# The last product of a hybrid decoder block: one more buffer at each step of its weight supply

## The chip, the cores and the metric

The kernel runs on one core of one Trainium2 chip. The metric is the device time of one execution in microseconds, and the time given is the median of several runs. Engines are named as the profile names them: PE (TensorE), DVE (VectorE), ACT (ScalarE), POOL (GpSimd) and SP (SyncE, which here only issues DMAs).

## What is computed

One decoder layer over 256 tokens and 2048 features in float32: three token mixers with gates, an output product `w_o`, and a feed-forward part. The stage that matters here is the last one of the reference:

```python
h = rms_norm(x, norm_ffn_pre[l])
u = causal_depthwise_conv(h @ w_up[l], ffn_conv_w[l], ffn_conv_b[l])
u_g, u_v = jnp.split(u, 2, axis=-1)
x = x + rms_norm((jax.nn.silu(u_g) * u_v) @ w_down[l], norm_ffn_post[l])
```

`w_up` is 2048 x 11264 and `w_down` is 5632 x 2048. "The up projection" is the product with `w_up`, "the last product" the one with `w_down`.

## The kernel before

**Numbers as pairs.** Each float32 weight is split into a rounded value and a rest: ACT writes the rounded one (`whi`, a copy to type fp32r), DVE subtracts it from the raw weight and writes the rest (`wlo`). A product of such pairs takes three matmuls: rounded by rounded, rest by rounded, rounded by rest. So every raw piece of 128 x 1024 weights goes by DMA into a raw buffer `wraw`, then through one ACT and one DVE instruction, and then feeds PE.

**The last product.** The 5632 rows of `w_down` are 44 tiles of 128. 24 of them (`PLAIN`) are multiplied as they are: a "plain" step loads one piece (1024 of the 2048 output columns), splits it, and issues 12 matmuls of 128x512. The other 20 form ten pairs (`EARLY`) that are multiplied with Strassen's scheme: a "quad" step loads two pieces `b` and `a`, forms a difference piece `t` and a half piece of further differences with DVE, splits all of these (three and a half pieces), and issues 7 x 3 = 21 matmuls. It does everything twice, once for each half of the output columns (`Pair(0)`, `Pair(1)`): 2 x (24 x 12 + 10 x 21) = 996 matmuls. A quad is 8 DVE instructions, 4 ACT instructions and 2 DMAs; a plain step is one of each.

**Order.** In the last product ACT and DVE run in the order in which the code issues their instructions (`fixed` chains each to the one before on its engine), and PE too (`in_line`). `high` is the ACT rounding, `rest` the DVE subtraction (both show as line L980, that of `fixed`; the matmuls are L1264). The surrounding tile framework orders the tail of the up projection against this chain. DMAs of weights are issued by SP in one queue, in order; an issue waits until the buffer that it fills has been read for the last time.

**Buffers.** The pool `P0` holds 5 raw buffers (`wraw`), 4 rounded ones (`whi`) and 4 rests (`wlo`), used in turn; the half piece of a quad has its own two tiles (`h4`, `l4`). A big tile with tag `hT` in `P0` holds first `hT`, then pieces of `w_o`, then `h2T` (the activations of the up projection, 16 x 2 x 256 numbers in each partition), and in the last product `fin`: the result rows, a row of gains, and two scratch pieces for `t`. The small tiles of the up projection's activation (`t`, `fs`, `fa`) lie in a pool `P2b`, which is closed at the end of the up projection; the pool `P2c` is opened in its place.

**Steps of the two halves.** With P a plain step and Q a quad, the loops before give for the first half PPPQ, nine times PPQ, and PPP. In the second half the last six plain pieces are kept: they are loaded and split early, but multiplied at the very end (K). Its order is PPP, the results of the first half, Q PQ PPQ PPQ PQ PPQK PPQK PQK PPQK PPQ KK, with weighing steps and a gain load between. The kept pieces of the quads go to tiles of the activations that are no longer read.

After the last product follow the row norm, the residual and the output DMAs.

Of the kernel before, what the change touches and what calls it, by code (L numbers as in the profile page):

```python
# [23 lines left out]
F32 = mybir.dt.float32  # L24
# [6 lines left out]
D = 2048  # L31
T = 256
# [3 lines left out]
EPS = 1e-6  # L36

EARLY = [(0, 1), (2, 3), (4, 5), (6, 7), (8, 9), (11, 12), (13, 14), (15, 16), (17, 18), (19, 20)]
PLAIN = [*range(22, 33), 10, 21, *range(33, NFT)]
BA, BB, BC, BG = 2100, 2200, 2200, 2500  # L40
PR = 1000
NW0, _ = 9, 6
# [12 lines left out]
def block(ctx: ExitStack, tc: tile.TileContext, x, xf, fp, cst, rows, sgw, w1, w2, wf_a, wt_bv, wf_bu, wf_c,  # L55
# [3 lines left out]

    PZ = ctx.enter_context(tc.tile_pool(name="pz", bufs=1))  # L60
    P0 = ctx.enter_context(tc.tile_pool(name="p0", bufs=1))
    PS = ctx.enter_context(tc.tile_pool(name="ps", bufs=4, space=PSUM))
    marks = set()

# [687 lines left out]
    class Unit:  # L752
# [251 lines left out]
    for cb in range(3):  # L1004
# [7 lines left out]
        if cb < 2:  # L1012
            for t in range(2):
                done_o(cb, t)
    h2k = P0.tile([128, 4, 2, 1024], R, tag="hT", name="h2k")
# [10 lines left out]
    for n, (cb, p) in enumerate(HELD):  # L1026
        for i in range(2):
            if n == 0 and i == 0:
                pe_last[0] = mm_o(cb, 1, p, held[n], (i,))
            else:  # L1030
                in_line(mm_o, cb, 1, p, held[n], (i,))
            if (n, i) == (3, 1):
                h2 = P0.tile([128, KT, 2, T], R, tag="hT", name="h2T")
            k = 2 * n + i - 7
            if k == 14:
                order_of(order2)
                fixed(S, S.activation, junk, po[3, 1], AF.Square, accum_out=ss1[1][:, 3:4])
            for k in ([k] if 0 <= k < 14 else [14, 15] if k == 14 else []):
                in_line(enter2, 0, k)
                if k % 4 == 3:  # L1040
                    up = wf_up[k // 8][:, k // 4 % 2 * 1024:k // 4 % 2 * 1024 + 1024]
                    if k < 15:
                        behind.append(tuple(order2))
                        ws2[k // 8].append(piece(up, 1024))
                    else:
                        raw = fetch(up, 1024)
        if p == 7 and cb == 2:
            done_o(cb, 1)
# [170 lines left out]
    turn = [0]  # L1219

    def scratch():
        turn[0] ^= 1
# [9 lines left out]
    def high(hi, x):  # L1232
        fixed(S, S.activation, hi, x, AF.Copy)

    def rest(lo, x, hi):
        fixed(V, V.tensor_sub, lo, x, hi.bitcast(F32))

    def weights(src, into=None):
        raw = fetch(src, 1024)
        hi, lo = (into[:, 0], into[:, 1]) if into is not None else ring(raw.name)  # L1240
        high(hi, raw)
        rest(lo, raw, hi)
        return hi, lo

    def ring(name):
        return [P0.tile([128, 1024], R, tag=tag, bufs=4, name=f"{tag}{name}") for tag in ("whi", "wlo")]

    class Pair:
        def __init__(self, p):
# [25 lines left out]

        def quad(self, j):

            k0, k1 = EARLY[j]
            last = j == len(EARLY) - 1
            b, a = (fetch(wt_dq[self.p, j][:, x:x + 1024], 1024) for x in (0, 1024))  # L1280
            L, U = slice(0, 512), slice(512, 1024)
            nm = f"q{self.p}_{j}"
            tt = scratch()
            (hb, lb), (ha, la), (ht, lt) = (ring(nm + x) for x in "bat")
            h4, l4 = (P2c.tile([128, 512], R, tag=tag, name=f"{tag}{nm}") for tag in ("h4", "l4"))
            high(hb, b)
            fixed(V, V.tensor_sub, tt[:, L], b[:, L], a[:, U])
# [3 lines left out]
            fixed(V, V.tensor_sub, tt[:, U], b[:, L], a[:, U])  # L1291
            high(ht, tt)
            rest(la, a, ha)
            fixed(V, V.tensor_sub, b[:, U], b[:, U], tt[:, U])
            high(h4[:, L], b[:, U])
            rest(lt, tt, ht)
            rest(l4[:, L], b[:, U], h4[:, L])
            sh, sl = sums_at(j)
            s1, s2, s4 = ((sh[:, i], sl[:, i]) for i in range(3))
            for bank_, act, (h, l), c in (  # L1300
                    (self.c[0][1], s4, (hb, lb), L), (self.c[0][0], g2(k1, H1), (hb, lb), U),
                    (self.p1, g2(k0, H1), (ha, la), L), (self.p5, s1, (ha, la), U),
                    (self.p7, g2(k0, H2), (ht, lt), L), (self.p6, s2, (ht, lt), U),
                    (self.c[1][0], g2(k1, H2), (h4, l4), L)):
# [34 lines left out]
    NP, NQ, KEEP = len(PLAIN), len(EARLY), 6  # L1339


    first, second = Pair(0), None
    i = 0
    for j in range(NQ):
        while i < 3 + (NP - 6) * j // (NQ - 1):
            first.plain(i)
            i += 1
        first.quad(j)
    for i in range(i, NP):
        first.plain(i)  # L1350
    first.combine()
    second = Pair(1)
    kept = []
    i = 0
    for j in range(NQ):
        while i < 3 + (NP - KEEP - 3) * j // (NQ - 1):
            second.plain(i)
            if i == 2:
                for t in range(2):
                    for n in range(2):  # L1360
                        first.result(t, n, fixed)
            elif 3 <= i < 7:
                first.weigh((i - 3) // 2, (i - 3) % 2, fixed)
            elif i == 9:
                nc.sync.dma_start(gain, row(3072, 1024))
            i += 1
        second.quad(j)
        if j == len(EARLY) - 1:
# [3 lines left out]
        for x in range(0 if j < NQ - 5 else 1 if j < NQ - 1 else KEEP - 4):  # L1372
            k = NP - KEEP + len(kept)
            into = None
            if j < NQ - 1:
                kt = P2.tile([128, 11, T], R, tag=("gh", "gl")[j % 2], bufs=4, name=f"kept{k}")
                into = kt[:, 0:8].rearrange("p (a b) c -> p a (b c)", a=2)
            kept.append((PLAIN[k], weights(wt_dn[1, k], into)))
    assert i == NP - KEEP and len(kept) == KEEP
    second.combine()  # L1380
    for t in range(2):
        for n in range(2):
# [21 lines left out]
def _layout(inp):  # L1404
# [66 lines left out]
    k0, k1 = [k for k, _ in EARLY], [k for _, k in EARLY]  # L1471
    quads = np.concatenate([dn[:, k1, 1], dn[:, k1, 0], dn[:, k0, 0], dn[:, k0, 1]], axis=3)


# [40 lines left out]
```

## Time and profile before

| | |
|---|---|
| median of 3 runs | 1578.02 us (1577.71 to 1579.3) |
| the profiled execution, its time | 1579.86 us |
| its span in the profile | 1578.1 us, 1.76 us less than its time |
| PE busy | 1565.3 us, 99% of the span |
| DVE busy | 1232.2 us, 78% |
| ACT busy | 891.5 us, 56% |
| granted TensorE clock | 0.998 of full |
| last product, first to last matmul issue | 1340.29 to 1568.72 us of the span |

The page gives shares over the whole span. Busy time of PE is the union of its matmuls, whose shown durations overlap, so a busy PE may still lose time between starts; start times tell that, busy shares do not. In rows of the timeline the first number is the start from the beginning of the span, the second the duration, and in brackets stands the idle time before it and what ended it.

### The profile page before, as it was taken

To read this page: it belongs to the slowest core of one execution; us is meant where nothing else is said; L and a number is where in the kernel's file an instruction comes from. 1 tells how busy PE (TensorE), PEld (TensorE's weight loads), DVE (VectorE), ACT (ScalarE), POOL (GpSimd) and SP (SyncE) were. 2 spreads that over 40 slices of the span, in tenths; PEclk is the share of its full clock that TensorE was granted. 3 is DMA by queue.
4 is the path that set the end of the run, shared out by engine and by line. 5 is a ranking of instruction groups with operands and counts; after the bars stand their busy time and mean duration, and the time that the engine had idled before them with its cause. 6 is when DMAs were issued, how large, how long until landed. Compare 5 with 4: busy or idle time off the path is not lost.

```text
span 1578.1 us, 22348 instructions
## 1 busy us (share of the span) xinstructions
PE 1565.3 (99%) x8173; PEld 1328.5 (84%) x8173; DVE 1232.2 (78%) x2114; ACT 891.5 (56%) x1442; POOL 20.1 (1%) x50
## 2 busy tenths in 40 slices
PE   9999999999999999999999999999999999999997
PEld 7888889888888787788888888888888888888875
DVE  7899999858866555465557988888777777998997
ACT  7644444447646675644456666565555555555653
POOL 1000020000000000000000000000000000000000
PEclk9999999999999999999999999999999999999999
DMA  9555556665765545456774666666666666666674
GB/s 366 190 182 186 187 179 206 197 194 182 232 202 160 153 141 174 160 186 187 241 249 146 208 194 186 191 188 187 189 189 191 190 189 191 197 209 203 213 228 159
DMA packets 85439, 307.94 MB, mean 195 GB/s; under 512 B 9808, under 2 KB 10832, under 8 KB 84304
## 3 DMA queue, kind: packets, MB, share of 16 engines
q1 hardware_dynamic: 83376, 297.84, 59.3%
q0 software_dynamic: 1520, 8.39, 1.5%
q8 instruction: 64, 1.05, 0.3%
q14 instruction: 47, 0.39, 0.1%
q10 hardware_dynamic: 432, 0.28, 0.1%
HBM read 301.23 MB, written 4.19 MB: 194 GB/s over the span
## 4 chain that ended last, share of the span: by engine, by line
PE 96%; DVE 2%; DMA 1%; issue 0%; ACT 0%; DVEq 0%; ACTq 0%
PE ps L172 29%; PE ps L179 15%; PE pg L193 6%; PE pg L192 6%; PE pg L194 6%; PE pd0b L1264 5%; PE pd1a L1264 4%; PE py L193 3%; PE py L194 3%; PE py L192 3%; PE po L192 2%; PE po L193 2%; PE po L194 2%; PE pd0a L1264 2%; PE pd1b L1264 1%; PE pv L192 1%
## 5 line engine op out<-in xcount | busy, mean ns | idle before, releaser
L144 DVE TENSOR_TENSOR wlo<-wraw,whi 128x1024 fp32r<-128x1024 f32 x440 | 535.6, 1220 | 174.6 <-ACT whi L143 167.8
L143 ACT ACTIVATE whi<-wraw 128x1024 fp32r<-128x1024 f32 x440 | 461.3, 1053 | 246.4 <-PE pg L194 98.2
L172 PE MATMUL ps<-h2T,whi 128*128 128x512 f32 x1360 | 325.0, 391 | 0.0
L172 PEld LDWEIGHTS ps<-h2T,whi 128*128 128x128 f32 x1360 | 249.8, 188 | 48.2
L179 PEld LDWEIGHTS ps<-h2T,wlo 128*128 128x128 f32 x1360 | 174.5, 191 | 6.7
L179 PE MATMUL ps<-h2T,wlo 128*128 128x256 f32 x1360 | 176.6, 283 | 0.0
L172 PE MATMUL ps<-hT,whi 128*128 128x512 f32 x640 | 157.0, 391 | 0.0
L214 ACT ACTIVATE t<-ps 128x256 f32<-128x256 f32 x125 | 47.6, 382 | 183.3 <-PE ps L172 182.9
L194 PE MATMUL pg<-whi,hT 128*128 128x512 f32 x384 | 150.9, 393 | 0.0
L193 PE MATMUL pg<-wlo,hT 128*128 128x512 f32 x384 | 150.7, 392 | 0.0
L192 PE MATMUL pg<-whi,hT 128*128 128x512 f32 x384 | 147.9, 393 | 0.0
L172 PEld LDWEIGHTS ps<-hT,whi 128*128 128x128 f32 x640 | 116.2, 188 | 21.4
L215 DVE TENSOR_TENSOR t<-ps,t 128x256 f32<-128x256 f32 x125 | 52.7, 422 | 68.8 <-ACT t L214 68.3
L475 DVE SCALAR_TENSOR_TENSOR cv<-hb,fps,cv 128x256 f32<-128x256 f32 x240 | 105.6, 479 | 0.0
L179 PEld LDWEIGHTS ps<-hT,wlo 128*128 128x128 f32 x640 | 84.4, 191 | 4.4
L179 PE MATMUL ps<-hT,wlo 128*128 128x256 f32 x640 | 86.5, 283 | 0.0
L193 PEld LDWEIGHTS pg<-wlo,hT 128*128 128x128 f32 x384 | 72.1, 188 | 16.2 <-issue 1.1
L194 PEld LDWEIGHTS pg<-whi,hT 128*128 128x128 f32 x384 | 72.1, 188 | 15.2 <-issue 0.7
L192 PEld LDWEIGHTS pg<-whi,hT 128*128 128x128 f32 x384 | 71.8, 188 | 14.7 <-issue 0.3
L980 DVE TENSOR_TENSOR wlowraw<-wraw,whiwraw 128x1024 fp32r<-128x1024 f32 x44 | 53.2, 1223 | 11.7 <-ACT whiwraw L980 10.3
L980 ACT ACTIVATE whiwraw<-wraw 128x1024 fp32r<-128x1024 f32 x44 | 45.7, 1054 | 18.1 <-PE pd0b L1264 14.9
L1194 ACT ACTIVATE fa<-fs,fps 128x256 f32<-128x256 f32 x88 | 52.5, 596 | 1.2 <-DVE fs L217 0.9
(1020 smaller groups left out, 2466.8 us busy)
## 6 DMA issues: line engine op xcount, KB each, us to landing
wraw<-in_wf_up_dram SPq DMA_DIRECT2D x176, 512.0 KB, 4.3
wraw<-in_wt_g_dram SPq DMA_DIRECT2D x96, 512.0 KB, 4.2
wraw<-in_wt_p_dram SPq DMA_DIRECT2D x48, 512.0 KB, 4.1
wraw<-in_wt_dn_dram SPq DMA_DIRECT2D x48, 512.0 KB, 4.2
wraw<-in_wt_dq_dram SPq DMA_DIRECT2D x40, 512.0 KB, 4.5
wraw<-in_wf_a_dram SPq DMA_DIRECT2D x32, 512.0 KB, 4.4
wraw<-in_wt_o_dram SPq DMA_DIRECT2D x32, 512.0 KB, 4.5
wraw<-in_wf_bu_dram SPq DMA_DIRECT2D x16, 512.0 KB, 4.3
```

The lines of the kernel that those rows point to most:

```text
L143: S.activation(hi[:, :n], raw[:, :n], AF.Copy)
L144: V.tensor_sub(lo[:, :n], raw[:, :n], hi[:, :n].bitcast(F32))
L172: ins = PE.matmul(ps[:, :, ts], lhsT=ws[k // 8][0][:, c:c + 128], rhs=mov[:, k, :, ts], start=(k == 0 and not t), stop=(k == n - 1), skip_ ...
L179: ins = PE.matmul(ps[:, 1, ts], lhsT=ws[k // 8][1][:, c:c + 128], rhs=mov[:, k, 0, ts], start=False, stop=False, skip_group_check=True).ins
L192: PE.matmul(ps, lhsT=xh, rhs=hi, start=first, stop=False)
L193: PE.matmul(ps, lhsT=xh, rhs=lo, start=False, stop=False)
L194: return PE.matmul(ps, lhsT=xl, rhs=hi, start=False, stop=last).ins
L215: V.tensor_add(t1 if rb is not None else dst, ps[:, 0], t1)
L475: V.scalar_tensor_tensor(ca[:, j], hb[:, j, k:k + T], w(j, k), ca[:, j], op0=ALU.mult, op1=ALU.add)
L980: seq[eng] = [op(*args, **kw).ins]
L1194: S.activation(a, s, AF.Identity, bias=fps[:, C_FB + f:C_FB + f + 1], scale=w[2])
L1264: ins = PE.matmul(bank, lhsT=a[x], rhs=w[y], start=first and j == 0, stop=last and j == 2).ins
```

## The change

1. The tag `hT` moves from `P0` to a pool `PH` of its own at the other end of the memory. That pool is closed after the up projection, and a pool `P2d` takes its place, with the results (`res`), the gains (`gain`), and three spare pieces `y0`, `y1`, `y2`.
2. The last product takes its buffers from cycles: raw pieces from the 5 of `wraw` and then `y2`, rounded ones from the 4 of `whi` and then `y0`, rests from the 4 of `wlo` and then `y1`. So there are 6 raw buffers, 5 rounded and 5 rests.
3. The two scratch pieces for `t` move from the `hT` tile to `P2c`, that is, to memory that `P2b` used.
4. The order of the steps is written out in two strings. In the first half one plain step moves from the end to before the fourth quad. In the second half plain steps move ahead: PPP, results, P Q PPQ PPQ PPQ PPQ PPQK PQK PQK PQK PQ KK.

The matmuls, their number, and the work of ACT and DVE per step are the same. The diff's core:

```diff
+PH_ctx = ExitStack()
+PH = PH_ctx.enter_context(tc.tile_pool(name="ph", bufs=1, side="right"))
...
-    hT = P0.tile([128, KT, 2, T], R, tag="hT", name="hT")
+    hT = PH.tile([128, KT, 2, T], R, tag="hT", name="hT")
...
     P2c = ctx.enter_context(tc.tile_pool(name="p2c", bufs=1))
-    fin = P0.tile([128, 7168], F32, tag="hT", name="fin")
-    res = fin[:, 0:4096].rearrange("p (t n) -> p t n", t=2)
-    gain = fin[:, 4096:5120]
...
-        return fin[:, 5120 + 1024 * turn[0]:6144 + 1024 * turn[0]]
+    PH_ctx.close()
+    P2d = ctx.enter_context(tc.tile_pool(name="p2d", bufs=1, side="right"))
+    res = P2d.tile([128, 2, D], F32, name="res")
+    gain = P2d.tile([128, 1024], F32, name="gain")
...
+    def spare(x):
+        return lambda name, dt=R: P2d.tile([128, 1024], dt, tag=f"y{x}", name=name)
+
+    def extra(x):
+        return lambda name, dt=R: P2c.tile([128, 1024], dt, tag=f"x{x}", name=name)
...
+    raws_of = cycle(tagged("wraw", 5, F32) + [spare(2)])
+    whi = cycle(tagged("whi", 4, R) + [spare(0)])
+    wlo = cycle(tagged("wlo", 4, R) + [spare(1)])
+    scratch = cycle([extra(0)] + [extra(1)])
...
+FIRST = "PPPQPPQPPQPPPQPPQPPQPPQPPQPPQPPQPP"
+SECOND = "PPPRRRRWPQWPPQWPWPQGPPQPPQPPQKPQKPQKPQKBPQKK"
```

In the strings R is a result step of the first half, W a weighing, G the second gain load, B the load of the residual rows.

**Where the two halves join the up projection.** The order of DVE at the end of the up projection is the first place where the programs differ. Before, from the first quad's first rest (`wloq0_0b`; `wloq0_0a` and `wloq0_0t` are the other two) to the last write of the activations (`gl3`); `t1_466`, `fs87`, `fa87` and `fa86` are the last activation tiles of the up projection, `fin` holds the difference piece:

```order
L980 TENSOR_TENSOR wloq0_0b_12926<-wraw470_12921,whiq0_0b_12925 128x1024
L215 TENSOR_TENSOR t1_466_12839<-ps466_12805,t1_466_12839 128x256
L980 TENSOR_TENSOR fin_12855<-wraw470_12921,wraw471_12923 128x512
L217 SCALAR_TENSOR_TENSOR fs87_12838<-t1_466_12839,rb2_7887 128x256
L980 TENSOR_TENSOR wloq0_0a_12928<-wraw471_12923,whiq0_0a_12927 128x1024
L980 TENSOR_TENSOR wraw470_12921<-wraw470_12921,fin_12855 128x512
L1195 SCALAR_TENSOR_TENSOR fa87_12843<-fs87_12838,fps_65,fa87_12843 128x255
L1196 SCALAR_TENSOR_TENSOR fa87_12843<-fs87_12838,fps_65,fa87_12843 128x254
L980 TENSOR_TENSOR wloq0_0t_12930<-fin_12855,whiq0_0t_12929 128x1024
L1199 TENSOR_TENSOR fa86_12789<-fa86_12789,fa87_12843 128x256
L1203 TENSOR_TENSOR gl3_7883<-fa86_12789,gh3_7879 128x256
```

And DVE with the change, at the same place (`u4`, `u5` are the raw pieces of the first quad, `t00` its difference piece, `lb00` and `la00` its rests; line numbers are 6 higher here):

```order
L221 TENSOR_TENSOR t1_466_12842<-ps466_12808,t1_466_12842 128x256
L223 SCALAR_TENSOR_TENSOR fs87_12841<-t1_466_12842,rb2_7890 128x256
L1201 SCALAR_TENSOR_TENSOR fa87_12846<-fs87_12841,fps_68,fa87_12846 128x255
L1202 SCALAR_TENSOR_TENSOR fa87_12846<-fs87_12841,fps_68,fa87_12846 128x254
L1205 TENSOR_TENSOR fa86_12792<-fa86_12792,fa87_12846 128x256
L1209 TENSOR_TENSOR gl3_7886<-fa86_12792,gh3_7882 128x256
L986 TENSOR_TENSOR t00_12933<-u4_12929,u5_12931 128x512
L986 TENSOR_TENSOR u5_12931<-u5_12931 128x512
L986 TENSOR_TENSOR lb00_12935<-u4_12929,hb00_12934 128x1024
L986 TENSOR_TENSOR t00_12933<-u4_12929,u5_12931 128x512
L986 TENSOR_TENSOR la00_12937<-u5_12931,ha00_12936 128x1024
```

The whole first quad now stands behind the tail of the up projection's activation, where the two were woven together.

**The end of the second half.** The loads in SP's queue, before (`in_wt_dn` is a plain or kept piece, `in_wt_dq` half of a quad; the two pairs of `in_wt_dq` are the ninth and the tenth quad):

```order
L103 DMA wraw543_14398<-in_wt_dn_dram 128x1024
L103 DMA wraw544_14402<-in_wt_dn_dram 128x1024
L103 DMA wraw545_14420<-in_wt_dn_dram 128x1024
L103 DMA wraw546_14438<-in_wt_dq_dram 128x1024
L103 DMA wraw547_14440<-in_wt_dq_dram 128x1024
L103 DMA wraw548_14484<-in_wt_dn_dram 128x1024
L103 DMA wraw549_14488<-in_wt_dn_dram 128x1024
L103 DMA wraw550_14506<-in_wt_dn_dram 128x1024
L103 DMA wraw551_14524<-in_wt_dq_dram 128x1024
L103 DMA wraw552_14526<-in_wt_dq_dram 128x1024
```

And with the change, the ninth and the tenth quad again, with what follows them:

```order
L1265 DMA u79_14460<-in_wt_dn_dram 128x1024
L1265 DMA u80_14464<-in_wt_dn_dram 128x1024
L1265 DMA u81_14482<-in_wt_dq_dram 128x1024
L1265 DMA u82_14484<-in_wt_dq_dram 128x1024
L1265 DMA u84_14536<-in_wt_dn_dram 128x1024
L1265 DMA u83_14529<-in_wt_dn_dram 128x1024
L1265 DMA u85_14554<-in_wt_dq_dram 128x1024
L1265 DMA u86_14556<-in_wt_dq_dram 128x1024
L1265 DMA u87_14600<-in_wt_dn_dram 128x1024
L1265 DMA u88_14606<-in_wt_dn_dram 128x1024
```

Ahead of each of the last quads there are now two loads of plain or kept pieces, where there were three: one plain step has left that place.

More of the change, by code (lines that the diff above doesn't have):

```diff
@@ L38 @@
 EARLY = [(0, 1), (2, 3), (4, 5), (6, 7), (8, 9), (11, 12), (13, 14), (15, 16), (17, 18), (19, 20)]
+LATE = []
 PLAIN = [*range(22, 33), 10, 21, *range(33, NFT)]
+PAIRS = EARLY + LATE
+FIRST = "PPPQPPQPPQPPPQPPQPPQPPQPPQPPQPPQPP"
+SECOND = "PPPRRRRWPQWPPQWPWPQGPPQPPQPPQKPQKPQKPQKBPQKK"
 BA, BB, BC, BG = 2100, 2200, 2200, 2500
@@ L1014, in block @@
                 done_o(cb, t)
-    h2k = P0.tile([128, 4, 2, 1024], R, tag="hT", name="h2k")
+    h2k = PH.tile([128, 4, 2, 1024], R, tag="hT", name="h2k")
     into = [h2k[:, i] for i in range(4)] + [None] * 4 + [s8([128, 2, 1024], R, f"kept{i}") for i in range(3)]
@@ L1032, in block @@
             if (n, i) == (3, 1):
-                h2 = P0.tile([128, KT, 2, T], R, tag="hT", name="h2T")
+                h2 = PH.tile([128, KT, 2, T], R, tag="hT", name="h2T")
             k = 2 * n + i - 7
@@ L1215, in block @@
     P2c = ctx.enter_context(tc.tile_pool(name="p2c", bufs=1))
-    fin = P0.tile([128, 7168], F32, tag="hT", name="fin")
-    res = fin[:, 0:4096].rearrange("p (t n) -> p t n", t=2)
-    gain = fin[:, 4096:5120]
-    turn = [0]
-    def scratch():
-        turn[0] ^= 1
-        return fin[:, 5120 + 1024 * turn[0]:6144 + 1024 * turn[0]]
+    PH_ctx.close()
+    P2d = ctx.enter_context(tc.tile_pool(name="p2d", bufs=1, side="right"))
+    res = P2d.tile([128, 2, D], F32, name="res")
+    gain = P2d.tile([128, 1024], F32, name="gain")
     ss3 = PZ.tile([128, 2, 8], F32, name="ss3")
@@ L1236, in rest, with cycle, take, tagged @@
         fixed(V, V.tensor_sub, lo, x, hi.bitcast(F32))
-    def weights(src, into=None):
[L1239 to L1246, printed above, removed]
+    def cycle(makers):
+        n = [0]
+        def take(name, *args):
+            n[0] += 1
+            return makers[(n[0] - 1) % len(makers)](name, *args)
+        return take
+    def spare(x):
+        return lambda name, dt=R: P2d.tile([128, 1024], dt, tag=f"y{x}", name=name)
+    def extra(x):
+        return lambda name, dt=R: P2c.tile([128, 1024], dt, tag=f"x{x}", name=name)
+    def tagged(tag, bufs, dtype):
+        return [lambda name, dt=dtype: P0.tile([128, 1024], dt, tag=tag, bufs=bufs, name=name)] * bufs
+    raws_of = cycle(tagged("wraw", 5, F32) + [spare(2)])
+    whi = cycle(tagged("whi", 4, R) + [spare(0)])
+    wlo = cycle(tagged("wlo", 4, R) + [spare(1)])
+    scratch = cycle([extra(0)] + [extra(1)])
+    count = [0]
+    def load(src, n=1024):
+        count[0] += 1
+        to = raws_of(f"u{count[0]}", F32)
+        nc.sync.dma_start(to[:, :n], src)
+        return to
+    def split(x, into=None):
+        hi, lo = into or (whi(f"h{count[0]}"), wlo(f"l{count[0]}"))
+        high(hi, x)
+        rest(lo, x, hi)
+        return hi, lo
+    def weights(src, into=None):
+        return split(load(src), into)
+    def fourth(tag):
+        return P2c.tile([128, 512], R, tag=tag, name=f"{tag}_{count[0]}")
     class Pair:
@@ L1276, in quad @@
         def quad(self, j):
-            k0, k1 = EARLY[j]
-            last = j == len(EARLY) - 1
-            b, a = (fetch(wt_dq[self.p, j][:, x:x + 1024], 1024) for x in (0, 1024))
+            b, a = (load(wt_dq[self.p, j][:, x:x + 1024]) for x in (0, 1024))
             L, U = slice(0, 512), slice(512, 1024)
[L1282 to L1285, printed above, removed]
+            t = scratch(f"t{self.p}{j}", F32)
+            (hb, lb), (ha, la), (ht, lt) = ((whi(f"h{x}{self.p}{j}"), wlo(f"l{x}{self.p}{j}")) for x in "bat")
+            h4, l4 = fourth("h4"), fourth("l4")
             high(hb, b)
-            fixed(V, V.tensor_sub, tt[:, L], b[:, L], a[:, U])
+            fixed(V, V.tensor_sub, t[:, L], b[:, L], a[:, U])
             fixed(V, V.tensor_sub, a[:, U], a[:, U], a[:, L])
@@ L1290, in quad, with seven @@
             rest(lb, b, hb)
-            fixed(V, V.tensor_sub, tt[:, U], b[:, L], a[:, U])
-            high(ht, tt)
+            fixed(V, V.tensor_sub, t[:, U], b[:, L], a[:, U])
+            high(ht, t)
             rest(la, a, ha)
[L1294 to L1297, printed above, removed]
+            fixed(V, V.tensor_sub, b[:, U], b[:, U], t[:, U])
+            high(h4, b[:, U])
+            rest(lt, t, ht)
+            rest(l4, b[:, U], h4)
+            self.seven(j, (hb, lb), (ha, la), (ht, lt), (h4, l4))
+        def seven(self, j, b, a, t, f):
+            k0, k1 = PAIRS[j]
+            last = j == len(PAIRS) - 1
+            L, U = slice(0, 512), slice(512, 1024)
             sh, sl = sums_at(j)
@@ L1300, in quad @@
             for bank_, act, (h, l), c in (
[L1301 to L1304, printed above, removed]
+                    (self.c[0][1], s4, b, L), (self.c[0][0], g2(k1, H1), b, U),
+                    (self.p1, g2(k0, H1), a, L), (self.p5, s1, a, U),
+                    (self.p7, g2(k0, H2), t, L), (self.p6, s2, t, U),
+                    (self.c[1][0], g2(k1, H2), f, L)):
                 side = any(bank_ is x for x in (self.p1, self.p5, self.p6, self.p7))
@@ L1337, in weigh, with keep @@
             do(V, V.tensor_mul, self.at(t, n), self.at(t, n), gain[:, n * 512:n * 512 + 512])
[L1339 to L1345, printed above, removed]
+    def keep():
+        n = len(kept)
+        into = None
+        if n < SECOND.count("K") - 2:
+            kt = P2.tile([128, 11, T], R, tag=("gh", "gl")[n % 2], bufs=4, name=f"kept{n}")
+            into = [kt[:, 4 * x:4 * x + 4].rearrange("p b c -> p (b c)") for x in range(2)]
+        k = SECOND.count("P") + n
+        kept.append((PLAIN[k], weights(wt_dn[1, k], into)))
+    first, kept = Pair(0), []
+    i = j = n = 0
+    for c in FIRST:
+        if c == "P":
             first.plain(i)
             i += 1
-        first.quad(j)
-    for i in range(i, NP):
-        first.plain(i)
+        else:
+            first.quad(j)
+            j += 1
     first.combine()
     second = Pair(1)
[L1353 to L1356, printed above, removed]
+    i = j = n = 0
+    for c in SECOND:
+        if c == "P":
             second.plain(i)
[L1358 to L1365, printed above, removed]
-            i += 1
-        second.quad(j)
-        if j == len(EARLY) - 1:
+            i += 1
+        elif c == "R":
+            first.result(n // 2, n % 2, fixed)
+            n += 1
+        elif c == "W":
+            first.weigh((n - 4) // 2, n % 2, fixed)
+            n += 1
+        elif c == "G":
+            nc.sync.dma_start(gain, row(3072, 1024))
+        elif c == "B":
             yb = s16(P0, [128, 2, D], F32, "yb")
@@ L1371, in block @@
                 G.dma_start(yb[:, t], kept_y[:, t])
[L1372 to L1379, printed above, removed]
+        elif c == "K":
+            keep()
+        else:
+            second.quad(j)
+            j += 1
     second.combine()
@@ L1470, in _layout @@
     plain = c(dn[:, PLAIN].transpose(0, 1, 3, 2, 4)).reshape(2, len(PLAIN), 128, 1024)
-    k0, k1 = [k for k, _ in EARLY], [k for _, k in EARLY]
+    k0, k1 = [k for k, _ in PAIRS], [k for _, k in PAIRS]
     quads = np.concatenate([dn[:, k1, 1], dn[:, k1, 0], dn[:, k0, 0], dn[:, k0, 1]], axis=3)
```

## The prediction

> **What bounds the kernel now.** I began with the page's busy times and its chain of work, then took PE's starts in the last product, then who waited for whom there. The page first:
>
> ```profile
> PE 1565.3 (99%) x8173; PEld 1328.5 (84%) x8173; DVE 1232.2 (78%) x2114; ACT 891.5 (56%) x1442; POOL 20.1 (1%) x50
> PE 96%; DVE 2%; DMA 1%; issue 0%; ACT 0%; DVEq 0%; ACTq 0%
> ```
>
> The chain is PE for 96% of the span, and the change leaves PE's work alone. So only PE's waits can be won, and only in the last product, since the instructions ahead of it stand in the same order. The table by stage for the matmuls of L1264, and PE's first and last row of them:
>
> ```profile
> 1340.20:1534.70 194.50, 194.41 (x858) 160.97 (x859) 1.00 0.66 213
> 1340.29 0.39 PE L1264 MATMUL pd0b<-whiwraw,gh 128*128 128x512 f32 x1
> 1568.72 0.39 PE L1264 MATMUL pd1a<-whiwraw,gl 128*128 128x512 f32 x1
> ```
>
> In the first 194.5 us 858 matmuls start, one every 226.7 ns at full clock: there PE never waits. At that pace the 996 matmuls take 995 x 0.22667 = 225.53 us from first to last start; they took 1568.72 - 1340.29 = 228.43. So PE loses **2.9 us**, all of it after 1534.7. That is 0.18% of the time and a ceiling on the gain. Two views say what was late, the waits of DVE in the last product and the chain in its last stretch:
>
> ```profile
> DVE wlowraw L980 <- ACT whiwraw L980: 8.6, 10, 1.3
> DVE fin L980 <- DMA wraw<-in_wt_dq_dram: 4.0, 2, 2.4
> ...
> 1526.34 0.69 DVE l4q L980
> ...
> 1527.05 5.79 DMA wraw<-in_wt_dq_dram
> ...
> 1539.59 4.91 DMA wraw<-in_wt_dq_dram
> ```
>
> DVE stood idle 4.0 us for two loads, one each for the ninth and the tenth quad of the second half. A quad's second piece could be issued only at 1527.05, when the quad before gave its raw buffer free, and took 5.79 us to land. (The 8.6 us of waits for ACT are DVE at the limit of its ring, ahead of PE.) DVE's own rows tell the pace:
>
> ```profile
> 1520.40 0.68 DVE L980 TENSOR_TENSOR fin<-wraw,wraw 128x512 f32<-128x512 f32 x1
> ...
> 1521.73 1.22 DVE L980 TENSOR_TENSOR wloq_7b<-wraw,whiq_7b 128x1024 fp32r<-128x1024 f32 x1
> ...
> 1523.47 1.22 DVE L980 TENSOR_TENSOR wloq_7a<-wraw,whiq_7a 128x1024 fp32r<-128x1024 f32 x1
> ...
> 1525.21 1.22 DVE L980 TENSOR_TENSOR wloq_7t<-fin,whiq_7t 128x1024 fp32r<-128x1024 f32 x1
> ...
> 1527.02 1.23 DVE L980 TENSOR_TENSOR kept<-wraw,kept 128x1024 fp32r<-128x1024 f32 x1
> 1528.16 2.35 DVE L980 TENSOR_TENSOR wlowraw<-wraw,whiwraw 128x1024 fp32r<-128x1024 f32 x2
> 1532.93 0.69 DVE L980 TENSOR_TENSOR fin<-wraw,wraw 128x512 f32<-128x512 f32 x1 [2.42 <-DMA wraw<-in_wt_dq_dram]
> ...
> 1544.60 0.69 DVE L980 TENSOR_TENSOR fin<-wraw,wraw 128x512 f32<-128x512 f32 x1 [1.62 <-DMA wraw<-in_wt_dq_dram]
> ```
>
> A quad costs DVE 1527.02 - 1520.40 = 6.62 us, a plain or kept piece 1528.16 - 1527.02 = 1.14. PE spends 21 x 0.22667 = 4.76 on a quad, 12 x 0.22667 = 2.72 on a plain step, nothing on a kept one until the end. So DVE gains on PE in PPQ (8.90 to 10.20) and falls behind in PQK (8.90 to 7.48, that is 1.42 us).
>
> **The change, part by part.**
>
> *Six raw buffers: -2.9 us at most.* With four loads to a PQK and six buffers, each of a quad's loads waits for the kept or plain piece of the quad before: between that release and the quad's first DVE instruction lie a quad and two pieces, 8.9 us. Before, it was the two plain pieces after 1527.02, some 3.5 us. The page's landing times:
>
> ```profile
> wraw<-in_wt_dn_dram SPq DMA_DIRECT2D x48, 512.0 KB, 4.2
> wraw<-in_wt_dq_dram SPq DMA_DIRECT2D x40, 512.0 KB, 4.5
> ```
>
> At a median of 4.5 and 5.79 on the chain, 8.9 us suffices. I take all 4.0 us of DVE's waits as gone.
>
> The Trainium skill, DMA: Bandwidth & Descriptors, Anatomy of one DMA, fits a load from the POOL queue as 2.0 us plus its bytes over 436 GB/s, an estimate of 3.2 us for 512 KB. By it a sixth raw buffer would bring nothing: the load of 1527.05 would be there at 1530.25, before DVE wants it. The rows with 5.79 and 4.91 us, on SP's queue with several loads under way, say otherwise.
>
> *Five rounded pieces and rests, and the order of the second half: +0.95 us left at the end.* A ring of five lets a plain piece be rounded as soon as PE is done with the piece five back. Take the two plain steps ahead of the sixth quad (`u67`, `u68`), where the K's begin. `u68` takes the buffer of the plain step ahead of the fifth quad; let PE be done with that one at T. ACT rounds (1.05 + 0.05), DVE starts on the rest at T + 1.10. From there DVE has 1.14 for it and four times Q K P of 6.62 + 1.14 + 1.14 = 8.90 each; the last plain rest (`u84`) is done at T + 1.10 + 1.14 + 35.60 + 0.08 + 0.04 = T + 37.96 (0.08 is what durations overlap, 1.22 less 1.14; 0.04 the hand to PE). PE comes to it after 166 matmuls, at T + 37.63. So PE waits 0.33 there. In the last quad `lt` is done 1525.21 + 1.22 - 1520.40 = 6.03 after DVE's start on it: T + 37.84 + 6.03 + 0.04 = T + 43.91. PE wants it after 190 matmuls, T + 43.07. That is 0.84 in all, and a matmul after a waited one comes 0.34 instead of 0.23 later:
>
> ```profile
> 1535.54 0.50 PE L1264 MATMUL pd1a<-wloq_8b,se 128*128 128x512 f32 x1 [0.37 <-DVE wloq_8b L980]
> 1535.88 0.39 PE L1264 MATMUL pd1a<-whiq_8b,se 128*128 128x512 f32 x1
> ```
>
> which makes 0.95. Bounds: 0, if DVE hands over faster by 0.2 us a block; 2.0, if one load costs DVE a further us.
>
> *The difference piece in `P2c`: +0.69 us at the join.* DVE can't start the first quad before the activation of the up projection has left `P2b`. The rows of that tail, ACT's first:
>
> ```profile
> 1341.50 0.37 ACT L214 ACTIVATE t<-ps 128x256 f32<-128x256 f32 x1
> 1344.34 0.60 ACT L1194 ACTIVATE fa<-fs,fps 128x256 f32<-128x256 f32 x1
> 1348.62 0.42 ACT L1202 ACTIVATE gh<-fa 128x256 fp32r<-128x256 f32 x1 [1.63 <-DVE fa L1199]
> ...
> 1342.95 0.42 DVE L215 TENSOR_TENSOR t<-ps,t 128x256 f32<-128x256 f32 x1
> 1343.89 0.42 DVE L217 SCALAR_TENSOR_TENSOR fs<-t,rb 128x256 f32<-128x256 f32 x1
> 1346.05 0.48 DVE L1195 SCALAR_TENSOR_TENSOR fa<-fs,fps,fa 128x255 f32<-128x255 f32 x1
> 1346.56 0.48 DVE L1196 SCALAR_TENSOR_TENSOR fa<-fs,fps,fa 128x254 f32<-128x254 f32 x1
> 1348.16 0.42 DVE L1199 TENSOR_TENSOR fa<-fa,fa 128x256 f32<-128x256 f32 x1
> 1349.07 0.43 DVE L1203 TENSOR_TENSOR gl<-fa,gh 128x256 fp32r<-128x256 f32 x1 [0.48 <-ACT gh L1202]
> ```
>
> Done one after the other from 1341.87: 0.42 + 0.42 + 0.60 + 0.48 + 0.48 + 0.42 + 0.42 + 0.43 = 3.67, and nine hand-overs of 0.04 (1348.58 to 1348.62 above) bring the first quad to 1345.90. By the offsets of the quad above its rests are ready 2.55, 4.29 and 6.03 later, plus 0.04: 1348.49, 1350.23, 1351.97. PE wants them at
>
> ```profile
> 1348.67 0.39 PE L1264 MATMUL pd0b<-wloq_0b,se 128*128 128x512 f32 x1
> ...
> 1350.03 0.39 PE L1264 MATMUL pd0a<-wloq_0a,gh 128*128 128x512 f32 x1
> ...
> 1351.39 0.39 PE L1264 MATMUL pd0a<-wloq_0t,gh 128*128 128x512 f32 x1
> ```
>
> so 0.58 late in all, with the extra 0.11 0.69. Bounds: 0.4 to 1.5, where the upper end has one more DVE instruction in front. The next plain step's rest is there at 1345.90 + 6.62 + 1.22 + 0.04 = 1353.78, ahead of PE (1348.67 + 4.76 + 0.69 = 1354.12), and PPQ gives 1.3 us back in each round, so this wait comes once.
>
> *At no cost:* the plain step moved in the first half (DVE had idle time for its ring at the passage between the halves, in the 8.6 us above); the spare buffers, which can be filled only after the last matmul of the up projection, where the gain load stood waiting before as well; `u6` behind that gain load in SP's queue, wanted some 10 us after its issue.
>
> *The sum* against the profiled execution: 1579.86 - 2.9 + 0.95 + 0.69 = **1578.6 us**. The median of the runs is 1578.02. The two late loads can explain why the profiled one is slower: without them PE's loss falls to between 0 and 0.3, 1577.0 to 1577.3, and runs of 1577.7 to 1579.3 lie between that and 1579.9. With the change little hangs on a load, so I expect the 1578.6 and less spread. To the median that is +0.04%. What a measurement of this kernel can tell from no change is about 0.2%, 3.2 us; more than PE's whole loss.
>
> **Rivals.**
>
> *All waits go: 1577.0.* The Trainium skill, Perfetto Trace Analysis, Optimization Strategy: the same gap coming back on the engine that should be saturated can mean that there are too few buffers for the next tile. As a mechanism here: DVE's hand-overs turn out 0.2 us a block shorter, and the tail of the up projection ends 0.7 sooner. For it speaks that DVE's waits before were waits for buffers; against, that DVE's rows leave no gap from 1520 on but those two, so that it is full and not starved.
>
> *Loads stay late where DVE is the bound: 1582.6, slower.* In the stretch T to T + 43.9 DVE has no slack, and each us that it waits for a load is one more of PE. The price is the old 4.0 us on top of the sum. It decides from 2.6 us of waiting, that is, loads of 11.5 us against 8.9. For it: 5.79 us with five loads under way, and now there are six; against: nothing above comes near.
>
> *The buffers bring nothing: 1580.6.* SP issues in order, and a load that stands behind another's wait comes as late as before; then the end of the second half stays as it is, and the join's 0.7 adds to it. Against it: the issues in the queue stand a quad further ahead of use.
>
> **The numbers.** My sum 0.70, all waits go 0.15, nothing 0.09, loads late 0.06. The bounds of the terms give 1577.4 to 1580.5 for the sum alone; with the first and third rival 1576.8 to 1580.6. Of the cases only the late loads end over 0.2% slower, with a little of the upper bounds; faster by 0.2% would need 1574.9, below PE's pace without any wait. Faster 0.03, same 0.90, slower 0.07.
>
> **What would show it.** DVE waits for `in_wt_dq` in the last product near 0 instead of 4.0 us. PE waits in the first quad for `la` and `lt`, some 0.6 us. PE's other waits at `u84` and the last quad, 0.9 us, with DVE without a gap for 40 us ahead of them. First to last matmul 227.2 us, not 228.4. I am wrong if PE waits elsewhere, above all at the passage between the halves, if a load still holds DVE up, or if the tail after the last matmul grows.

## The result and the profile after

| | before | after |
|---|---|---|
| median of 5 runs | 1577.76 us (1577.7 to 1579.3) | **1592.7 us** (1592.44 to 1594.28) |
| ratio | | 1.0095, 95% interval 1.0083 to 1.0106 |
| profiled execution: time, span | 1579.86, 1578.1 us | 1594.17, 1592.5 us |
| granted TensorE clock | 0.998 | 0.998 |

The change made the kernel 14.9 us slower. The forecast was 1578.6 us, no change. The page after, busy times and chain:

```profile
PE 1580.7 (99%) x8173; PEld 1326.4 (83%) x8173; DVE 1233.6 (77%) x2114; ACT 892.0 (56%) x1442; POOL 19.7 (1%) x50
PE 95%; DVE 3%; issue 1%; ACT 0%; DMA 0%; DVEq 0%; ACTq 0%
```

As many matmuls as before (8173), PE 99% busy as before and longer busy by 15.4 us. So PE does not wait more: it takes longer for the same matmuls. Where, the starts of the stages tell. Before, the first and the last matmul of the gates' product (tile `pg`) and the first of the up projection (`ps` from `h2T`); where the last product starts and ends is shown in the prediction, 1340.29 and 1568.72:

```profile
301.39 0.40 PE L192 MATMUL pg<-whi,hT 128*128 128x512 f32 x1
...
745.86 0.39 PE L194 MATMUL pg<-whi,hT 128*128 128x512 f32 x1
...
866.65 0.39 PE L172 MATMUL ps<-h2T,whi 128*128 128x512 f32 x1
```

After, the same three, then the first and the last matmul of the last product:

```profile
304.02 0.39 PE L198 MATMUL pg<-whi,hT 128*128 128x512 f32 x1
...
754.78 0.39 PE L200 MATMUL pg<-whi,hT 128*128 128x512 f32 x1
...
875.87 0.40 PE L178 MATMUL ps<-h2T,whi 128*128 128x512 f32 x1
...
1354.58 0.40 PE L1296 MATMUL pd0b<-h,gh 128*128 128x512 f32 x1
...
1582.98 0.39 PE L1296 MATMUL pd1a<-h,gl 128*128 128x512 f32 x1
```

Up to the gates 2.63 us are lost; in the gates 450.76 against 444.47, 6.29; between gates and up projection 0.30; in the up projection 478.71 against 473.64, 5.07; in the last product 228.40 against 228.43, nothing; behind it 9.52 against 9.38, 0.14. Together 14.4, the difference of the spans. The last product, the only place that the prediction looked at, starts 14.29 us late and takes as long as before.

How PE gets slower shows where one counts its matmuls in a fixed stretch. The columns are the stretch, its length, PE's busy time with the number of matmuls, the granted clock, DMA's share, GB/s. Before, 300 us of the gates and 400 us of the up projection:

```profile
400.00:700.00 300.00, 300.00 (x1512) 1.00 0.56 175
900.00:1300.00 400.00, 400.00 (x2303) 1.00 0.61 189
```

And after:

```profile
400.00:700.00 300.00, 300.00 (x1493) 1.00 0.55 173
900.00:1300.00 400.00, 400.00 (x2276) 1.00 0.61 188
```

PE is busy for the whole of both and the clock is full, but it gets 19 and 27 matmuls fewer done. The Trainium skill, Perfetto Trace Analysis, Identifying the Most-Contended Engine, warns that the busy share of matmuls is a poor measure of how close PE is to its limit, because they are pipelined; this trace agrees, 300.00 and 400.00 us in both kernels.

Which matmuls are slower, the groups tell (busy time, mean ns of one). Before:

```profile
L172 PE MATMUL ps<-h2T,whi 128*128 128x512 f32 x1360 | 325.0, 391 | 0.0
L179 PE MATMUL ps<-h2T,wlo 128*128 128x256 f32 x1360 | 176.6, 283 | 0.0
L194 PE MATMUL pg<-whi,hT 128*128 128x512 f32 x384 | 150.9, 393 | 0.0
L194 PE MATMUL py<-whi,Ct 128*128 128x512 f32 x64 | 25.0, 391 | 0.0
```

And after:

```profile
L178 PE MATMUL ps<-h2T,whi 128*128 128x512 f32 x1360 | 331.4, 395 | 0.0
L185 PE MATMUL ps<-h2T,wlo 128*128 128x256 f32 x1360 | 175.3, 281 | 0.0
L200 PE MATMUL pg<-whi,hT 128*128 128x512 f32 x384 | 152.8, 398 | 0.0
L200 PE MATMUL py<-whi,Ct 128*128 128x512 f32 x64 | 25.0, 391 | 0.0
```

Here every 128x512 group with a tile of the tag `hT` takes 4 to 5 ns longer, whether that tile is the moving operand (`ps`) or the stationary one (`pg`); the 128x256 one became 2 ns shorter; `py`, which reads no such tile, stands as it was. So the suspicion fell on the one part of the change that the prediction had not priced: `hT` lies elsewhere. The framework had it at byte 28160 of each partition before, a multiple of 256, and has it at 196576 now, 224 past one.

### The profile page after: what moved, and what is told of

Its sections match the earlier page's. It is cut to its first block, busy times and chain, and to the rows that moved or that the text cites. A ratio compares the mean times of both kernels' runs of the same rounds, so it can differ in the third digit from the quotient of the medians.

```text
span 1592.5 us, 22360 instructions
## 1 busy us (share of the span) xinstructions
PE 1580.7 (99%) x8173; PEld 1326.4 (83%) x8173; DVE 1233.6 (77%) x2114; ACT 892.0 (56%) x1442; POOL 19.7 (1%) x50
## 4 chain that ended last, share of the span: by engine, by line
PE 95%; DVE 3%; issue 1%; ACT 0%; DMA 0%; DVEq 0%; ACTq 0%
PE ps L178 29%; PE ps L185 15%; PE pg L199 6%; PE pg L198 6%; PE pg L200 6%; PE pd0b L1296 5%; PE pd1a L1296 4%; PE py L199 3%; PE py L200 3%; PE py L198 3%; PE po L200 2%; PE po L199 2%; PE po L198 2%; PE pd0a L1296 2%; PE pv L198 1%; PE pv L200 1%
## 5 line engine op out<-in xcount | busy, mean ns | idle before, releaser
L178 PE MATMUL ps<-h2T,whi 128*128 128x512 f32 x1360 | 331.4, 395 | 0.0
L200 PE MATMUL pg<-whi,hT 128*128 128x512 f32 x384 | 152.8, 398 | 0.0
L198 PE MATMUL pg<-whi,hT 128*128 128x512 f32 x384 | 149.9, 398 | 0.0
L986 DVE TENSOR_TENSOR l<-u,h 128x1024 fp32r<-128x1024 f32 (+1 forms) x64 | 66.5, 1055 | 14.4 <-ACT h L986 14.4
L986 ACT ACTIVATE h<-u 128x1024 fp32r<-128x1024 f32 (+1 forms) x64 | 56.5, 920 | 28.9 <-DVE u L986 13.3
```

The lines of the kernel that those rows point to most:

```text
L178: ins = PE.matmul(ps[:, :, ts], lhsT=ws[k // 8][0][:, c:c + 128], rhs=mov[:, k, :, ts], start=(k == 0 and not t), stop=(k == n - 1), skip_ ...
L198: PE.matmul(ps, lhsT=xh, rhs=hi, start=first, stop=False)
L200: return PE.matmul(ps, lhsT=xl, rhs=hi, start=False, stop=last).ins
L986: seq[eng] = [op(*args, **kw).ins]
```

## The experiments

The figures in ns below are mean distances from one matmul's start to the next, worked out from the traces (waits of over 300 ns left out). "Up" stands for the up projection, which has `h2T` as moving operand and a weight as stationary one: for each tile of its result 8 matmuls of 128x512, 16 of 128x256, and again 8 of 128x512. The first of its two figures is for 128x512, the second for 128x256. "Gates" are the 128x512 matmuls with `hT` as stationary operand and a weight as moving one. Before: up 228.4 and 119.5, gates 227.8; after: 233.0 and 118.6, gates 233.2. In the runs of the experiments single executions of the kernel before took 1576.0 to 1580.3 us, so a median is good to about a microsecond.

**The move alone.** The kernel before, with the four uses of the tag in the new pool:

```diff
-    hT = P0.tile([128, KT, 2, T], R, tag="hT", name="hT")
+    hT = PH.tile([128, KT, 2, T], R, tag="hT", name="hT")
... (h2k, h2T and fin likewise)
```

> The kernel before with only the tag hT (hT, h2k, h2T and at the end fin) in the pool at the other end of the memory; every engine's instructions stand in the order of before, with four rounded buffers and rests and five raw ones. There hT starts at byte 196576 of each partition, 32 past a multiple of 64; before at 28160, a multiple of 512; wraw stays, whi and wlo move down by 32768. Theory (hT's new start makes each matmul that reads it slower, by some 6 ns of 227): the whole loss comes from the move, which then costs a little more than the 14.9 us, since the waits of the last product stay as before: 1593 to 1595 us, 128x512 matmuls with h2T start to start at 233 ns instead of 228. Rival (the loss lies in the buffers, their cycles or the new order of the steps): 1577.8 us and 228 ns, as before.

1592.14 us, ratio 1.0089 (1.0075 to 1.0103); up 233.0 and 118.6, gates 233.2. The theory holds: the move alone costs 14.0 of the 14.9 us. It came out a microsecond below the expected 1593 to 1595.

**The change with 32 bytes more.** A small tile at the end of each closing pool:

```diff
+    PH.tile([128, 8], F32, name="hpad")
...
+    P2d.tile([128, 8], F32, name="ypad")
```

> The changed kernel with one tile of 32 bytes more at the end of each of the two closing pools, which moves hT from byte 196576 to 196544 (a multiple of 64) and the spare pieces y0, y1, y2 as well; nothing else differs, and the order is that of the changed kernel. Theory A (it is the start, 32 past a multiple of 64): the 15 us go away and what is left is the change in the last product, 1.4 us less waiting of PE than before: 1576.5 us (1576 to 1578.6), 128x512 matmuls with h2T at 228 ns. Theory B (it is the place, the far end of the memory or its distance from the weights): 1592.7 us and 233 ns, as without the 32 bytes.

1578.2 us, ratio 1.0003 (0.9994 to 1.0012). The loss is gone with 32 bytes, at the same end of the memory: theory B falls, as far as it blames that end. But theory A did not come out as written either, 1.7 us above its 1576.5 and with another pattern: up 233.0 and 113.7, gates 229.3. So the time is that of before because a gain and a loss cancel: from first to last matmul start the up projection takes 1.7 us less than before, the gates 1.9 us more. Its counts, more in the up projection than before and fewer in the gates:

```profile
400.00:700.00 300.00, 300.00 (x1508) 1.00 0.56 176
900.00:1300.00 400.00, 400.00 (x2308) 1.00 0.62 190
```

**The kernel before with `hT` 32 bytes further up.**

```diff
+    P0.tile([128, 8], F32, name="padA")
     hT = P0.tile([128, KT, 2, T], R, tag="hT", name="hT")
+    P0.tile([128, 8], F32, name="padB")
```

> The kernel before with 32 unused bytes ahead of the tile hT and 32 behind it, in the same pool: hT moves from byte 28160 to 28192, 32 past a multiple of 64, and whi, wlo and all behind by 64 (to multiples of 64). Order as before. Theory A (the start): as slow as the changed kernel or a little more, 1593 to 1595 us, h2T's 128x512 matmuls at 233 ns. Theory B (the place): 1577.8 us, 228 ns. Should whi and wlo at multiples of 64 that are not of 512 cost something too, it is over 1595.

1594.03 us, ratio 1.0101 (1.0087 to 1.0115), up 233.0 and 118.6, gates 233.2. So 32 bytes ahead of `hT` and 32 behind it (which move the weights by 64) are enough to spoil the kernel before, with no other buffer, no other order and no other end of the memory:

```profile
400.00:700.00 300.00, 300.00 (x1493) 1.00 0.55 173
900.00:1300.00 400.00, 400.00 (x2279) 1.00 0.60 187
```

**Everything but the move.** No closing pools: `hT` in `P0`, and the results, gains, both difference pieces and the sixth raw buffer cut from its tile in the last product, the fifth rounded piece and rest in `P2c`:

```diff
-    P2d = ctx.enter_context(tc.tile_pool(name="p2d", bufs=1, side="right"))
...
+    fin = P0.tile([128, 8192], F32, tag="hT", name="fin")
...
-        return lambda name, dt=R: P2d.tile([128, 1024], dt, tag=f"y{x}", name=name)
+        return lambda name, dt=R: P2c.tile([128, 1024], dt, tag=f"y{x}", name=name)
```

> The changed kernel without its closing pools: hT, h2k and h2T stay in P0 at byte 28160 as before, the results, the gains, the sixth raw buffer and the two difference pieces are cut from that tile in the last product, and the fifth rounded buffer and rest lie in P2c. Six raw, five rounded and rests and the new order of the steps stay. Theories A and B alike (the move did the harm): PE's waits of the last product are all that changes, 1576 to 1578.6 us. Rival (the buffers or the order): 1592.7 us.

1578.32 us, ratio 0.9997 (0.9988 to 1.0005), all paces of before. The buffers and the order do no harm, and they bring nothing that the whole time shows.

**How far does it matter?** The kernel before again, `hT` moved by 64, 128, 256 and 512 bytes, and what lies behind it by 512:

```diff
+    P0.tile([128, 16], F32, name="padA")       # 32, 64, 128 in the others
     hT = P0.tile([128, KT, 2, T], R, tag="hT", name="hT")
+    P0.tile([128, 112], F32, name="padB")      # 96, 64, none
```

> The kernel before with hT 64 bytes further up (64 unused bytes ahead, 448 behind, so that all behind moves by 512): hT at byte 28224, a multiple of 64 but not of 128. The changed kernel with 32 bytes more had its hT at 196544, 448 past a multiple of 512, and showed h2T's 128x512 matmuls at 233.1 ns (before: 228.5) but its 128x256 ones at 113.7 (before: 119.5). Theory A1 (every multiple of 64 does that): the same two paces here, the up projection 471.7 us from first to last matmul start instead of 473.4, in all 1576 us. Theory A2 (64 is the granule, and 448 of 512 matters only by its neighbourhood to the weights): paces of before, 1578 us. Either way nothing near the 15 us.

> The kernel before with hT 128 bytes further up, at 28288, all behind by 512. If 128 is the granule, paces as before (228.5 and 119.5 ns for h2T's 128x512 and 128x256 matmuls, 1578 us); if only multiples of 512 are special, those of the changed kernel with 32 bytes more (233.1 and 113.7 ns, 1576 us).

> The kernel before with hT 256 bytes further up, at 28416, all behind by 512. If 128 or 256 is the granule, paces as before (228.5 and 119.5 ns, 1578 us); if only multiples of 512 are special, 233.1 and 113.7 ns, 1576 us.

> The kernel before with hT and all tiles behind it 512 bytes further up: hT at 28672, which is a multiple of 2048, where 28160 is 1536 past one. If only the place within 512 bytes counts, as before (228.5 and 119.5 ns, 1578 us). If a 128x512 matmul, which reads 2048 bytes in a row of each partition, gains by not crossing a multiple of 2048, its pace goes to 226.7 ns or below and the time to 1574 or less.

| `hT` moved by | time, us | ratio | up, ns | gates, ns |
|---|---|---|---|---|
| 64 | 1578.99 | 1.0008 (0.9999 to 1.0018) | 229.3, 115.6 | 233.3 |
| 128 | 1590.9 | 1.0085 (1.0070 to 1.0100) | 232.7, 118.7 | 232.6 |
| 256 | 1577.67 | 1.0001 (0.9991 to 1.0010) | 228.4, 119.5 | 227.7 |
| 512 | 1578.41 | 1.0003 (0.9994 to 1.0012) | 228.4, 119.5 | 227.8 |

256 and 512 change nothing, which fits a pattern that repeats after 256 bytes. 128 is nearly as bad as 32, which none of the theories so far said: for 128 they gave 1576 or 1578 us. 64 has paces that neither A1 nor A2 named. Its counts show two effects of opposite sign, in the gates and in the up projection:

```profile
400.00:700.00 300.00, 300.00 (x1496) 1.00 0.55 174
900.00:1300.00 400.00, 400.00 (x2326) 1.00 0.61 191
```

Set side by side by the role of `hT`, the runs agree. With `hT` at 64, its matmuls are fast where it is moving (229.3) and slow where it is stationary (233.3); with `hT` at 192 (the change with 32 bytes more) it is the reverse, 233.0 and 229.3. The weights lie at multiples of 256 in these runs. Take the moving operand's start less the stationary one's: at 64 the up projection has 64 and the gates -64, which is 192; at 192 they have 192 and 64. Then 64 is good and 192 bad for the 128x512 matmuls in both. So it may not be the start of `hT` that counts, but the two operands' starts against each other. In the run with 32 bytes ahead of `hT` the weights had moved by 64, so its difference was 224, the changed kernel's own; its paces are equal to the changed kernel's.

**Both operands moved.** That theory (R) makes a strange forecast: leave `hT` where the change puts it, and displace everything else to match.

```diff
+    P0.tile([128, 56], F32, name="padA")
     idn = P0.tile([128, 128], F32, name="idn")
```

> The changed kernel with 224 unused bytes at the start of P0 and nothing else: hT stays at byte 196576 and the spare pieces at 217056 and up, all 224 past a multiple of 256, and now whi, wlo, the activations and every other operand of PE in P0, P1 and P2 are 224 past one as well. Theory R (what counts is the moving operand's start less the stationary one's, modulo 256; the runs so far: 0 fast, 64 and 192 about as fast, 32, 128 and 224 slow): the difference is 0 everywhere, as in the kernel before, so h2T's matmuls come at 228.4 (128x512) and 119.5 ns (128x256), the last product takes 227.0 us from first to last matmul start instead of 228.4, in all 1577 us. Rival (the start itself counts, and 224 past a multiple of 256 is a bad one): still 233 ns, now also for the matmuls that read no hT, the 996 of the last product among them, so 1592.7 us plus some 6 ns for each of those, over 1600 us.

1577.45 us, ratio 0.9999 (0.9990 to 1.0008); up 228.4 and 119.5, gates 227.8, and the counts are those of the kernel before:

```profile
400.00:700.00 300.00, 300.00 (x1512) 1.00 0.56 176
900.00:1300.00 400.00, 400.00 (x2303) 1.00 0.61 190
```

The operands now start 224 past a multiple of 256, an odd multiple of 32, and the kernel is as fast as with all at multiples of 256. Theory R holds here, and a rule on the start alone falls. The Trainium skill, TensorE: Matmul & The Clock Gate, Step-by-step: what each phase is for, says that PE reads its moving and its stationary operand through two independent ports of SBUF, and that loading the next weights takes no read bandwidth from the running matmul. By that one would not expect the starts of the two to matter to each other; here they do, 228 against 233 ns, and the measurement decides.

The spare pieces `y0` and `y1` are a second instance. In the change they are moving operands at 224, the activations stationary ones at 0. In 180 us of the last product without a wait, after and then in this run:

```profile
1370.00:1550.00 180.00, 180.00 (x790) 1.00 0.67 215
```

```profile
1353.00:1533.00 180.00, 180.00 (x796) 1.00 0.68 216
```

Six matmuls at 0.2267 us are 1.4 us, lost by buffers that the prediction had under "at no cost". The starts show where. In the first half each quad takes one piece in `y0` and `y1`. In the nine quads after the first, the six matmuls on that piece come every 233.7 ns in the changed kernel, and the next five, on a piece at 0, still every 231.5; the matmuls ahead of it keep 226.7. With both operands moved all of them come every 226.6 to 226.8. So a matmul with the difference 0 is slow too when it follows such a piece.

**All differences in one trace.** The kernel before, block k of `h2T` starting 16 k past a multiple of 256:

```diff
-                h2 = P0.tile([128, KT, 2, T], R, tag="hT", name="h2T")
+                h2 = P0.tile([128, KT, 2 * T + 4], R, tag="hT", name="h2T")[:, :, 0:2 * T]
+                h2 = h2.rearrange("p k (a t) -> p k a t", a=2)
```

> The kernel before with 16 unused bytes behind each of the 16 blocks of h2T, so that block k starts at 16 k modulo 256 and all 16 differences to the weights (which are at 0) stand in one trace; tiles behind move by 256. Theory R, from the runs with one difference each: 128x512 matmuls of block 0 at 228, block 4 at 229, blocks 2, 8, 12 and 14 at 233 ns; 128x256 ones of block 0 at 119.5, block 4 at 115.6, block 8 at 118.7, block 12 at 113.7, block 14 at 118.6; the other blocks are new. Rival (the pace hangs on the tile as a whole and not on each matmul's own operand): all blocks alike. The time is somewhere between 1576 and 1588 us.

One execution, 1579.77 us. Mean ns by block, over 84 tiles of the product:

| block | 0 | 1 | 2 | 3 | 4 | 5 | 6 | 7 |
|---|---|---|---|---|---|---|---|---|
| 128x512 | 232.3 | 226.0 | 234.9 | 227.6 | 231.6 | 232.5 | 235.0 | 225.8 |
| 128x256 | 117.5 | 120.0 | 120.8 | 117.5 | 119.2 | 117.5 | 120.8 | 119.2 |

| block | 8 | 9 | 10 | 11 | 12 | 13 | 14 | 15 |
|---|---|---|---|---|---|---|---|---|
| 128x512 | 231.7 | 230.8 | 228.3 | 224.2 | 228.4 | 234.2 | 232.5 | 230.9 |
| 128x256 | 120.0 | 116.7 | 118.3 | 117.5 | 121.7 | 119.2 | 121.7 | 119.1 |

The blocks differ, each by about 1 ns or less from tile to tile, so the rival falls: the pace is not one of the tile as a whole. (In time the order in a tile is blocks 0 to 7 of 128x512, 0 to 15 of 128x256, 8 to 15 of 128x512.) But the values written down beforehand do not come back: block 0 has 232.3 instead of 228, block 4 231.6 instead of 229, block 12 228.4 instead of 233. In a mixed sequence a matmul's own difference does not give its pace. That what ran before counts, the matmuls behind the spare pieces showed; whether that explains these values, no run tells.

**The part that is free.** Only `h2T` 64 bytes further up, in the variant without closing pools, so that the up projection has the difference 64 and the gates keep 0:

```diff
-                h2 = P0.tile([128, KT, 2, T], R, tag="hT", name="h2T")
+                h2 = P0.tile([128, KT * 2 * T + 64], R, tag="hT", name="h2T")[:, 16:16 + KT * 2 * T]
+                h2 = h2.rearrange("p (k a t) -> p k a t", k=KT, a=2)
```

> The variant of the changed kernel without closing pools, with h2T alone 64 bytes further up (its tile 256 bytes longer, so that all behind stays at the same place modulo 256). By the run with hT 64 further up in the kernel before, the pair of a 128x512 and a 128x256 matmul of the up projection takes 344.9 ns instead of 347.9, the up projection 469.2 us instead of 473.4 from first to last matmul start, while the gates' product with hT, which lost 6.5 us there, keeps its hT where it was. Theory R: 1578.3 - 4.2 = 1574.1 us, a ratio of 0.997 to the kernel before. If the loads of the stationary side or DVE take the gain back, 1576 to 1578.

**1572.45 us, ratio 0.9962 (0.9949 to 0.9976)**: 5.3 us or 0.38% faster than the kernel before, and a little more than forecast. Gates as before, up projection 17 matmuls ahead in 400 us:

```profile
400.00:700.00 300.00, 300.00 (x1512) 1.00 0.56 175
900.00:1300.00 400.00, 400.00 (x2320) 1.00 0.62 191
```

From first to last matmul start the up projection takes 469.2 us instead of 473.4, the 4.2 expected; the last product takes 227.0 (before: 227.6 to 229.3 over the traces that have its code). Against the variant without closing pools the medians differ by 5.9 us and the profiled spans by 3.9 (1576.6 and 1572.7); single executions of that variant ran from 1576.6 to 1579.4 us, so the part beyond 4.2 is not shown to be an effect.

**The order alone.** In the variant without closing pools only the new order is left, with 5 raw, 4 rounded and 4 rest buffers:

```diff
-    raws_of = cycle(tagged("wraw", 5, F32) + [extra(2)])
-    whi = cycle(tagged("whi", 4, R) + [spare(0)])
-    wlo = cycle(tagged("wlo", 4, R) + [spare(1)])
+    raws_of = cycle(tagged("wraw", 5, F32))
+    whi = cycle(tagged("whi", 4, R))
+    wlo = cycle(tagged("wlo", 4, R))
```

> The variant without closing pools with five raw buffers and four rounded ones and rests, as before; only the new order of the steps is left of the change. The prediction's theory (the buffers take the waits away): DVE waits for loads of quads 4 us or more in the last product, since the second load of a quad again waits for the raw buffers of the quad before, and the runs PQK of the new order give it less time than PPQK did; from first to last matmul start of the last product 228 to 230 us, where the variant with the buffers took 227.0 and the kernel before 228.4. Rival (the order does it, the buffers nothing): 227.0 to 227.4 us, loads of quads waited for 1.2 us. In all 1577 to 1580 us.

One execution, 1577.74 us; the last product took 228.2 us, within the range of the prediction's theory. The reason given there was wrong, though: no load of a quad is among the waits of DVE in this trace, so the five raw buffers were enough in this order. What PE waits for instead is a rest that comes late, twice; here, and below it the same variant with all the buffers (the columns: us in total, times, longest):

```profile
PE pd1a L1293 <- DVE l L984: 1.1, 2, 0.6
```

```profile
PE pd1a L1293 <- DVE l L984: 0.4, 1, 0.4
```

With all the buffers these waits are shorter, and the last product takes 227.0 instead of 228.2 us, one execution each. Which of the three added buffers does it, no run separates.

## Why the prediction was wrong

**The step that failed** is in the first part: "the change leaves PE's work alone. So only PE's waits can be won, and only in the last product, since the instructions ahead of it stand in the same order". The order is the same and the work is the same, but its pace is not. The move of the tag `hT`, the first item of the change, has no term in the sum and no rival. It costs what the experiment with the move alone shows, 14 us, and 32 unused bytes at its end of the memory, or 224 at the other, take that away. The up projection's 128x512 matmuls went from 228.4 to 233.0 ns, the gates' from 227.8 to 233.2. Nor did the range reach it: it was built from the waits alone, with PE's pace taken as given.

**The loads.** "DVE waits for `in_wt_dq` in the last product near 0 instead of 4.0 us": right but for one. After:

```profile
DVE l L986 <- ACT h L986: 14.4, 11, 1.7
...
DVE t L986 <- DMA u<-in_wt_dq_dram: 1.2, 1, 1.2
```

It is in the first half, and PE does not wait there. But "six raw buffers" was the wrong name for the cause: in the one trace with the order alone these waits are gone too. And the 2.9 us of loss that stood as the ceiling was one execution's: in the other traces with the last product of before, DVE waited 3.2 to 5.6 us for loads and PE lost 2.1 to 3.7 (227.6 to 229.3 us from first to last start). The least and the most of those waits, in the runs with `hT` moved by 128 and by 32:

```profile
DVE fin L982 <- DMA wraw<-in_wt_dq_dram: 3.2, 2, 2.1
```

```profile
DVE fin L982 <- DMA wraw<-in_wt_dq_dram: 5.6, 4, 2.0
```

**The join, +0.69.** Right in mechanism: after, the starts put `la` 0.14 and `lt` 0.24 us late, 0.38 together where 0.58 was forecast. The slower matmul came behind each of the two and was priced once, so the 0.60 in all is nearer to 0.69 than its parts are. The run with both operands moved shows the same.

**The end, +0.95.** Right in mechanism, near in size: with both operands moved, `u84` comes 0.58 us late (0.33 forecast), the rests of the last quad 0.32 (0.51), with two slower matmuls, one of which was priced, 1.12. In the changed kernel itself it is 0.79; slower matmuls on `y0` and `y1` leave DVE more time, which would explain that.

**"At no cost".** The plain step and the gain load were free, no wait of PE stands at either; the spare buffers were not, 1.4 us by their place.

**The last product as a whole,** forecast at 227.2 us: 227.4 with both operands moved, 227.0 without closing pools, 228.4 as changed, where the spare pieces take back what the waits gave. **The sum** of 1578.6 fits the variants without the loss: 1578.3 us without closing pools, 1577.5 with both operands moved. (The 1578.2 with 32 bytes more is a gain and a loss that cancel.) That proves little, as the kernel before takes 1577.8 to 1578.2 as well: the whole time cannot tell these terms from nothing, only the starts can. The rival "all waits go" is refuted by them, since `u84` and the last quad still wait in both.

What stays open is why PE's pace depends on the two starts, and what it would be for a given sequence. That the loads of the stationary operand and the reads of the moving one meet in the memory fits what was seen, but no run shows it.

## What to carry to other kernels

When tiles move, compare the byte at which each operand of PE starts, before and after: here the moving operand's start less the stationary one's, modulo 256, was worth 1% of the whole time, and a few unused bytes set it. Look for it with a count of matmuls in a fixed stretch, as PE's busy share and the clock show nothing. A change of place is a change for every instruction that reads the tile, however early it runs and however far from what the change is meant for.

## What the hardware showed unexpectedly

- With the same work, order and clock, 128x512 matmuls came every 226.7 to 228.4 ns at a difference of 0, 229 at 64, and 233 at 32, 128, 192 and 224. The 128x256 ones went otherwise: 119.5 at 0, 118.6 at 128 and 224, 115.6 at 64, 113.7 at 192. A pair of both was fastest at 64 (344.9 ns), not at 0 (347.9).
- Starts need not be multiples of 64 or 256 for that: with all operands at 224 past a multiple of 256 the pace was that of all at 0.
- A slow pair of starts is felt after it: five 128x512 matmuls behind a spare piece came every 231.5 ns though the difference of their own operands was 0 (first half of the last product, after).
- In the mixed sequence the 128x512 matmuls of one block came every 224.2 ns in the mean, below the 226.7 that the prediction had taken as PE's pace.
